# A bias table built in the middle of a down projection, and shorter steps of a layer norm

## The chip, the cores and the metric

The kernel runs on one core of a Trainium2 chip. The metric is the device time of one execution in microseconds (us), as the median of several runs. Engines are named as in the profile: PE (TensorE matmuls; PEld is its weight load), DVE (VectorE), ACT (ScalarE), POOL (GpSimd) and SP (SyncE, which issues most DMAs; a q behind an engine's name means its queue of DMA issues).

## The reference

One inference step of a two-layer encoder over 1056 tokens (1024 of a prompt, 32 of a stream) of width 1024. Layer 0 mixes with an mLSTM, layer 1 with attention over chunks of 64 tokens and the 8 chunks before each; both end in a squared-ReLU MLP of width 4096. Each half layer is

```
x <- LayerNorm(ALPHA * x + gate * sublayer(x * (1 + scale) + shift))
```

with scale, shift and gate from a product of a conditioning vector with w_ada (adaLN). The attention of layer 1 adds a relative-position bias, read for each of 16 heads out of a table of 257 values:

```
rel = q_off + jnp.arange(tq)[:, None] - jnp.arange(tk)[None, :]
idx = jnp.clip(rel, -MAX_REL, MAX_REL) + MAX_REL
return table[:, idx].astype(jnp.float32)
```

## The kernel before, in words

**Matmuls.** Weights are split into a high and a low part, and each product is three matmuls (L118, L119, L120; L120 takes the weight's low part). Raw weights come by SP into a ring of three raw buffers (`raw_tile`, L84), ACT casts the high part (L89), DVE subtracts to get the low part (L90).

**Blocks.** Tokens are worked in three blocks, ti = 0, 1, 2, of 384, 384 and 288 tokens.

**The first down** is layer 0's second MLP product, at about 860 to 1232 us of the span. It runs over groups g = 0 to 7 of the hidden width; w_dn_g_f is a weight quarter of a group, and dn_g_fc_t0 is the result for one of 8 column blocks and one token block. One quarter serves two column blocks, 72 matmuls. DVE adds each result to the residual ACX (L1051).

**Beside it** runs `ada_rest` (L1582), which forms layer 1's adaLN vectors on DVE: `ada_wide` loads 1 MB tiles radw by SP and multiplies them into aw (L279 for the first, L277 for the others), transposes (L286) and reduces (L288). At its very end it calls `bias_table` (L346): load the table (tab), reverse and scale it into rev on ACT and DVE, store rev into the DRAM buffer e_d, and store from there a (16, 64, 576) array of shifted rows into the DRAM buffer bias_d, which the attention reads. tab and rev are raw buffers.

**Order.** Such side tasks are Python generators; each yields the microseconds that should go by until its next step, and `Flow` lets them go on as the main stage emits its matmuls. A scheduler then sets the order on each engine. An engine works its list in order, and so does SP with its DMA issues.

**Layer 1's first norm** (`norm`, L907) follows the attention's output projection op_b, which takes the blocks in the order 2, 1, 0. For each block, sums (s_n, sr_n) go through a matmul with ones (mean_n, L929), the mean is subtracted (L942), squares are summed (q_n, qr_n) and go through a second such matmul (var_n, L929), and from it comes the scale w_n (L954 to L959), with which the block is scaled (L961) and modulated (L904 to L909). `norm` yields w[0] before the mean and w[1] before the variance. For layer 1's first norm w is taken from W10 (L884) by `end_out1` (L1983). The weights of layer 1's up projection (w_up) are split beside it.

Of the kernel before, what the change touches and what calls it, by code (L numbers as in the profile page):

```python
# [16 lines left out]
D = 1024  # L17
# [58 lines left out]
def trunk_kernel(ctx: ExitStack, tc: tile.TileContext, a, o):  # L76
    nc = tc.nc
    flow = Flow()
# [5 lines left out]
    def raw_tile(shape, name):  # L84
        return ring.tile(shape, F32, tag="raw", name=name, bufs=3)
# [55 lines left out]
    e_d = dr.tile([16, 640], F32, name="e_d")  # L141
    bias_d = dr.tile([16, 64, 576], F32, name="bias_d")
# [14 lines left out]
    def lng(i):  # L157
        return pt1[:, i * KC:(i + 1) * KC]

    def lnb(i):  # L160
        return pt1[:, 32 + i * KC:32 + (i + 1) * KC]
# [3 lines left out]
    def ada_part(l, i):  # L165
        return ada[:, l * 48 + i * KC:l * 48 + (i + 1) * KC, :]
# [141 lines left out]
    def ada_fix(base, parts):  # L308

        for i, kind in parts:  # L310
            ap = ada[:, base + i * KC:base + (i + 1) * KC, :]
            if kind == "sc":
                nc.vector.tensor_scalar_add(ap, ap, 1.0)
            else:
                nc.vector.tensor_scalar(ap, ap, 1.0, 1.0 / ALPHA, op0=ALU.add, op1=ALU.mult)

    def combine(ni, g, b, sc, sh):

        for cnd in range(2):
            nc.vector.tensor_mul(comb[:, ni, :, 0, cnd], g, sc[:, :, cnd])  # L320
            nc.vector.tensor_mul(comb[:, ni, :, 1, cnd], b, sc[:, :, cnd])
            nc.vector.tensor_add(comb[:, ni, :, 1, cnd], comb[:, ni, :, 1, cnd], sh[:, :, cnd])
# [20 lines left out]
        nc.vector.tensor_copy(hist, tp[:, :24].rearrange("p (j k) -> p k j", j=3))  # L343
        nc.vector.tensor_copy(n0c, tp[:, 24:28])

    def bias_table():  # L346

        tab = raw_tile([16, 257], "tab")
        nc.sync.dma_start(tab, a["rel_bias_b"][0])
        rev = raw_tile([16, 640], "rev")  # L350
        nc.vector.memset(rev[:, 639:640], 0.0)
        nc.scalar.activation(rev[:, 0:447], tab[:, 256:257].broadcast_to([16, 447]), AF.Copy, scale=8.0)
        fwd = tab[:, 65:257]
        nc.vector.tensor_scalar(rev[:, 447:639], bass.AP(fwd.tensor, fwd.offset + 191, [fwd.ap[0], [-1, 192]]),
                                8.0, None, op0=ALU.mult)
        nc.sync.dma_start(e_d, rev)

        nc.sync.dma_start(bias_d, bass.AP(e_d.tensor, e_d.offset + 63, [[640, 16], [-1, 64], [1, 576]]))


    up_cm = tc.tile_pool(name="upool", bufs=1, side="right", reuse_waits="tile")
# [506 lines left out]
    def acc_dma(d, x, out=False):  # L868
        for i in range(0, KC, 4):
            p = [d[:, i:i + 4], x[:, i:i + 4]]  # L870
            nc.sync.dma_start(*(p if out else reversed(p)))
# [7 lines left out]
    ADA_W = (4.5, 4.5, 2.0)  # L879
# [1 line left out]
    TAIL = (1.0, 1.5)  # L881
    W00 = (6.0, 12.0, 0.0, 0.0, 0.0, 3.0)
    W01 = ((4.0, 6.0, 1.0, 1.0, 1.0), (6.0, 8.0, 2.0, 2.0, 2.0), (3.0, 6.0, 0.0, 0.0, 0.0))
    W10 = ((10.0, 12.0, 0.0, 0.0, 0.0, 3.0), (16.0, 14.0, 0.0, 0.0, 0.0, 3.0))  # L884

    def make_layer(acc, pp, uo, cut=None):

# [654 lines left out]
    fwd, rev = (0, 1, 2), (2, 1, 0)  # L1542
# [10 lines left out]
    mm, norm, _, out_proj, _, add_gated_at = make_layer(acc, bank, uap)  # L1553
    combine(0, lng(0), lnb(0), ada_part(0, 4), ada_part(0, 3))
    norms = {}
# [24 lines left out]
        yield from ada_cols(a["w_ada_kv"], 0, 96, 8, mm, tmp_t, ADA_B)  # L1580

    def ada_rest():  # L1582
        yield from ada_wide(a["w_ada"][1], 0, 48, 48, mm, tmp_t, wc_tile, ADA_W)
        yield from ada_wide(a["w_ada_kv"], D, 104, 8, mm, tmp_t, wc_tile, ADA_W)
        ada_fix(48, [(1, "sc"), (2, "g"), (4, "sc"), (5, "g")])
        ada_fix(96, [(1, "sc")])
        combine(1, lng(1), lnb(1), ada_part(1, 1), ada_part(1, 0))
        combine(2, lng(2), lnb(2), ada_part(1, 4), ada_part(1, 3))
        yield
        bias_table()  # L1590

    class L0:
        wups = wup0
# [41 lines left out]
        def down():  # L1635
            flow.finish(norms["ada"])
            norms["ada"] = flow.add(ada_rest(), carry=True)
# [141 lines left out]
    for i, (nb, ns) in enumerate(((3, 0), (3, 0), (2, 1), (0, 3))):  # L1779
        bt = ring.tile([P, 2112], F32, tag="wc", name=f"bias{i}", bufs=6)  # L1780
        b3 = bt[:, :nb * 576].rearrange("p (b j) -> p b j", j=576) if nb else None
        for hd in range(2 if nb else 0):
            h0 = 2 * len(bias) + hd
            nc.sync.dma_start(b3[64 * hd:64 * hd + 64], bias_d[h0:h0 + 2 * nb - 1:2].rearrange("h i j -> i h j"))
        s3 = bt[:, nb * 576:nb * 576 + ns * 544].rearrange("p (b j) -> p b j", j=544) if ns else None
        for r in range(4 if ns else 0):
            h0 = 4 * len(sbias) + r
# [173 lines left out]
    def open_u2(pr):  # L1961
        u2_cm.append(tc.tile_pool(name=f"u2p{pr}", bufs=1, side="right", reuse_waits="tile"))
        u2p[pr] = u2_cm[-1].__enter__()
        u2[pr] = u2p[pr].tile([P, 2, KC, 2 * QN], F32R, tag="u2", name=f"u2_{pr}")

    def u2ap(hl, k, t0, n):
# [5 lines left out]
    mm, norm, norm_out, out_proj, gain_shift, add_gated_at = make_layer(  # L1972
        acc, lambda name: psD.tile([P, 512], F32, tag="mm", name=name, bufs=8), u2ap, 2 * QN)
# [6 lines left out]

    def end_out1(ti):
        t0, n = TBS[ti]
        norms[ti] = flow.add(norm(ti, 2, f"n10_{ti}", W10[ti == rev[-1]], True, lambda ti: acc_dma(  # L1983
            xsp[2][:, :, t0:t0 + n], acc[ti], True)), now=NOW)
        qo_cm[ti].__exit__(None, None, None)
        if ti == 1:
            open_u2(0)
# [6 lines left out]
    def early_up(ti, pr):  # L1994

        if ti == rev[-1] and pr:
            wup1[FIRST[pr - 1]] = up_weights(1, FIRST[pr - 1])
    out_proj([(0,), (1, 2, 3)], rev, wo_get, o_mov, ada_part(1, 2), end_out1, "b", width=[384, 384, 320],
             after_pr=early_up)

# [96 lines left out]
```

## Time and profile before

| | |
|---|---|
| median of 3 runs | 2435.93 us (2434.0 to 2439.79) |
| profiled execution, own time | 2433.89 us |
| its span | 2432.1 us |
| mean granted TensorE clock | 0.993 |
| busy PE, DVE, ACT, POOL | 97%, 81%, 48%, 7% of the span |
| first down's last groups | PE idle 2.03 us in 1180 to 1232 us |
| layer 1's first norm | PE idle 4.20 us in 1690 to 1730 us |

A row of the timeline has the start in us, the duration in us, the engine, the line, the operation, what it writes and reads with the shapes, and how many such are merged; in brackets stands the idle time before it and what ended it. A row of the waits has who waited for whom, the total in us, how often, and the longest. In the view of DMAs, "under 512 B" and so on count packets by size, and q1 is SP's ring.

### The profile page before, as it was taken

Reading aid. Unit: us, or ns where it says so; the run is one execution under the profiler, and the core shown is the slowest. Engines: PE = TensorE matmul, PEld = TensorE weight load, DVE = VectorE, ACT = ScalarE, POOL = GpSimd, SP = SyncE. Lnnn points to the kernel's source line nnn. Section 1 sums busy time; section 2 is a strip of 40 time slices with the busy share of each in tenths; the row PEclk is TensorE's granted clock in tenths of the full one; section 3 lists DMA queues with packets and bytes.
Section 4 is the critical chain, followed back from the end, with each engine's and each line's share of the span. In section 5 each row is a group of like instructions: output and inputs, shape, how many; then the busy total and the mean of one; then the engine's idle time right before and its main releaser. Section 6 shows DMA issues by size and latency. Waiting matters only on the chain.

```text
span 2432.1 us, 44293 instructions
## 1 busy us (share of the span) xinstructions
PE 2361.3 (97%) x17180; PEld 2265.0 (93%) x17180; DVE 1973.5 (81%) x4094; ACT 1179.6 (48%) x2394; POOL 166.8 (7%) x315
## 2 busy tenths in 40 slices
PE   7999999999999999999999989999999999899997
PEld 4999999999999999999989977889999999899997
DVE  4898997778788789999697666755998888887778
ACT  4654456377666620010157566763776777222212
POOL 0211100000000000000001134420000000000003
PEclk9999999999999999999999999999999999999999
DMA  8433323436556897656423220051486779966642
GB/s 296 122 112 96 101 88 99 143 114 219 179 188 192 294 346 265 234 203 231 145 67 95 74 64 1 15 135 32 163 282 229 256 259 339 364 243 232 227 151 72
DMA packets 283702, 423.60 MB, mean 174 GB/s; under 512 B 15320, under 2 KB 205164, under 8 KB 278372
## 3 DMA queue, kind: packets, MB, share of 16 engines
q1 hardware_dynamic: 279460, 390.50, 48.1%
q10 hardware_dynamic: 4032, 30.28, 3.1%
q8 instruction: 135, 2.21, 0.4%
q14 instruction: 75, 0.61, 0.1%
HBM read 304.91 MB, written 118.17 MB: 174 GB/s over the span
## 4 chain that ended last, share of the span: by engine, by line
PE 48%; DVE 12%; ACT 4%; DMA 3%; issue 2%; POOL 0%; SPq 0%; DVEq 0%; ACTq 0%; POOLq 0%
PE dn L1421 11%; PE up L1286 8%; PE dn L120 5%; PE dn L119 5%; PE dn L118 5%; PE pv L1859 3%; PE s L1802 2%; PE pt L1837 2%; DVE wf_u L90 1%; DVE HL L90 1%; DMA rdn_u<-in_w_up_dram 1%; PE op_b L118 1%; PE op_b L119 1%; PE op_b L120 1%; PE q L119 1%
## 5 line engine op out<-in xcount | busy, mean ns | idle before, releaser
L1051 DVE SCALAR_TENSOR_TENSOR ACX<-dn,ada,ACX 128x264 f32<-128x264 f32 (+6 forms) x664 | 281.8, 447 | 87.9 <-PE dn L1421 42.5
L1421 PE MATMUL dn<-fx,wf_d 128*128 128x264 f32 x2016 | 255.3, 286 | 6.0 <-DVE ACX L1051 3.7
L1421 PEld LDWEIGHTS dn<-fx,wf_d 128*128 128x128 f32 x2016 | 250.2, 189 | 8.1 <-DVE ACX L1051 2.3
L89 ACT CAST w_dn<-raw_dn 128x1024 fp32r<-128x1024 f32 x36 | 37.7, 1051 | 282.8 <-DVE aw L277 159.5
L118 PE MATMUL dn<-hs,w_dn 128*128 128x384 f32 (+2 forms) x512 | 161.3, 315 | 0.8 <-DVE ACX L1051 0.7
L119 PE MATMUL dn<-hs,w_dn 128*128 128x384 f32 (+2 forms) x512 | 160.9, 315 | 0.0
L120 PE MATMUL dn<-hs,w_dn 128*128 128x384 f32 (+2 forms) x512 | 155.9, 314 | 1.8 <-DVE w_dn L90 1.8
L1286 PE MATMUL up<-TF,wf_u 128*128 128x264 f32 x1056 | 143.4, 285 | 3.0 <-ACT H L1289 3.0
L1286 PE MATMUL up<-U,wf_u 128*128 128x264 f32 x1056 | 139.6, 285 | 1.5 <-DVE H L1292 1.1
L1286 PE MATMUL up<-u,wf_u 128*128 128x264 f32 x1056 | 139.7, 285 | 1.2 <-ACT wf_u L89 0.6
L277 DVE SCALAR_TENSOR_TENSOR aw<-radw,cs,aw 128x512 f32<-128x512 f32 x196 | 139.5, 744 | 0.0
L1286 PEld LDWEIGHTS up<-TF,wf_u 128*128 128x128 f32 x1056 | 134.3, 188 | 4.1 <-ACT H L1289 4.0
L1286 PEld LDWEIGHTS up<-U,wf_u 128*128 128x128 f32 x1056 | 133.0, 188 | 2.6 <-DVE H L1292 1.9
L1286 PEld LDWEIGHTS up<-u,wf_u 128*128 128x128 f32 x1056 | 132.6, 188 | 2.2 <-ACT wf_u L89 0.8
L119 PE MATMUL dn<-U,w_dn 128*128 128x384 f32 (+2 forms) x416 | 129.8, 313 | 0.0
L118 PE MATMUL dn<-U,w_dn 128*128 128x384 f32 (+2 forms) x416 | 129.3, 311 | 0.0
L120 PE MATMUL dn<-U,w_dn 128*128 128x384 f32 (+2 forms) x416 | 125.5, 312 | 0.6 <-DVE w_dn L90 0.6
L120 PEld LDWEIGHTS dn<-hs,w_dn 128*128 128x128 f32 x512 | 95.8, 188 | 2.9 <-DVE w_dn L90 2.6
L118 PEld LDWEIGHTS dn<-hs,w_dn 128*128 128x128 f32 x512 | 96.4, 188 | 1.4 <-DVE ACX L1051 1.0
L119 PEld LDWEIGHTS dn<-hs,w_dn 128*128 128x128 f32 x512 | 96.4, 188 | 0.0
L1812 DVE CUSTOM_DVE_ANT_0 p<-s,bias 128x576 f32<-128x576 f32 (+9 forms) x132 | 79.0, 606 | 19.6 <-PE s L1802 12.8
L90 DVE TENSOR_TENSOR HL<-H,HL 128x1056 fp32r<-128x1056 f32 x64 | 80.2, 1254 | 17.5 <-ACT HL L89 17.4
(394 smaller groups left out, 7163.4 us busy)
## 6 DMA issues: line engine op xcount, KB each, us to landing
hpl<-HL SPq DMA_DIRECT2D x144, 264.0 KB
rdn_u<-in_w_up_dram SPq DMA_DIRECT2D x64, 512.0 KB
hd<-HL SPq DMA_DIRECT2D x28, 1056.0 KB
fx<-hd SPq DMA_DIRECT2D x50, 528.0 KB
radw<-in_w_ada_dram SPq DMA_DIRECT2D x24, 1024.0 KB
hd<-HM SPq DMA_DIRECT2D x28, 792.0 KB
raw_up<-in_w_up_dram SPq DMA_DIRECT2D x40, 512.0 KB
raw_dn<-in_w_down_dram SPq DMA_DIRECT2D x36, 512.0 KB
```

The lines of the kernel that those rows point to most:

```text
L90: (eng or nc.vector).tensor_sub(dst_l, src, dst_h.bitcast(F32))
L118: nc.tensor.matmul(ps, wh, mov(0, k), start=(k == 0), stop=False)
L119: nc.tensor.matmul(ps, wh, mov(1, k), start=False, stop=False)
L120: nc.tensor.matmul(ps, wl, mov(0, k), start=False, stop=(k == nk - 1))
L277: nc.vector.scalar_tensor_tensor(acc[cnd], raw[:, k], sc, acc[cnd], op0=ALU.mult, op1=ALU.add)
L1051: nc.vector.scalar_tensor_tensor(xs, ps[:, off + o:off + o + mm_], gate[:, fc, cnd:cnd + 1], xs, op0=ALU.mult, op1=ALU.add)
L1286: nc.tensor.matmul(p, self.ws[w][:, wl, k], moving(f, tp, xl, k), start=first and k + n_ == 0, stop=k == 3 and n_ == 2, skip_group_check=n ...
L1421: nc.tensor.matmul(p, ws[w][:, wl, k], t[:, s0, xl], start=first and k + n_ == 0, stop=k == kg - 1 and n_ == 2, skip_group_check=not first)
L1802: nc.tensor.matmul(s[:, b, :w], qst, kk[i][:, g, k0 + j0:k0 + j0 + w], start=(i == 0), stop=(i == 1))
L1812: nc.vector.tensor_tensor_reduce(out=z.rearrange("p (b w) -> p b w", b=np_), in0=s[:, :np_, :w], in1=bt.rearrange("p (b w) -> p b w", b=np ...
L1837: nc.tensor.transpose(pt[:kp, j - j0, pr * P:(pr + 1) * P], ps_[pr][:, j * P:j * P + kp], ident)
L1859: nc.tensor.matmul(pv[64 * e:64 * e + 64, :nq], V[:kp, vt0 + j, g * 64:(g + 1) * 64], pts[e][:kp, j, :nq], start=(j == 0), stop=(j == nt - 1))
```

## The change

`ada_rest` now forms layer 1's 48 adaLN columns in two calls of `ada_wide` with `bias_table` between them, which puts the table into the middle of the first down. `bias_table` is a generator with yields, takes tab and rev from the pool of temporary tiles instead of the raw ring, and stores bias_d in four DMAs of four heads. W10 has an entry for each block: block 0 keeps its steps, block 1 goes from (10, 12) to (9, 10), and block 2 from (10, 12) to (6, 8). Lines behind L358 move by two or three.

```diff
-    def bias_table():
+    def bias_table(tmp_f):
 
-        tab = raw_tile([16, 257], "tab")
+        tab = tmp_f([16, 257], "tab")
         nc.sync.dma_start(tab, a["rel_bias_b"][0])
-        rev = raw_tile([16, 640], "rev")
+        yield 2.0
+        rev = tmp_f([16, 640], "rev")
...
         nc.sync.dma_start(e_d, rev)
-
-        nc.sync.dma_start(bias_d, bass.AP(e_d.tensor, e_d.offset + 63, [[640, 16], [-1, 64], [1, 576]]))
+        for h0 in range(0, 16, 4):
+            yield 1.0
+            nc.sync.dma_start(bias_d[h0:h0 + 4], bass.AP(e_d.tensor, e_d.offset + 640 * h0 + 63,
+                                                         [[640, 4], [-1, 64], [1, 576]]))
...
-    W10 = ((10.0, 12.0, 0.0, 0.0, 0.0, 3.0), (16.0, 14.0, 0.0, 0.0, 0.0, 3.0))
+    W10 = ((16.0, 14.0, 0.0, 0.0, 0.0, 3.0), (9.0, 10.0, 0.0, 0.0, 0.0, 3.0), (6.0, 8.0, 0.0, 0.0, 0.0, 3.0))
...
     def ada_rest():
-        yield from ada_wide(a["w_ada"][1], 0, 48, 48, mm, tmp_t, wc_tile, ADA_W)
+        yield from ada_wide(a["w_ada"][1], 0, 48, 24, mm, tmp_t, wc_tile, ADA_W)
+        yield from bias_table(tmp_t)
+        yield from ada_wide(a["w_ada"][1], 3 * D, 72, 24, mm, tmp_t, wc_tile, ADA_W)
         yield from ada_wide(a["w_ada_kv"], D, 104, 8, mm, tmp_t, wc_tile, ADA_W)
...
-        yield
-        bias_table()
...
-        norms[ti] = flow.add(norm(ti, 2, f"n10_{ti}", W10[ti == rev[-1]], True, lambda ti: acc_dma(
+        norms[ti] = flow.add(norm(ti, 2, f"n10_{ti}", W10[ti], True, lambda ti: acc_dma(
```

What the change does to the order is shown at three places. The first is SP's list around groups 3 and 4 of the first down. A row has the line, the operation, what is written and read (a tile's name ends in a number of the program), and the shape. Before:

```order
L96 DMA raw_dn_3_2_11898<-in_w_down_dram 128x4x256
L261 DMA radw_28_1_11808<-in_w_ada_dram 128x4x512
L261 DMA radw_32_0_11892<-in_w_ada_dram 128x4x512
L96 DMA raw_dn_3_3_12013<-in_w_down_dram 128x4x256
L261 DMA radw_32_1_12005<-in_w_ada_dram 128x4x512
L96 DMA raw_dn_4_0_12114<-in_w_down_dram 128x4x256
L261 DMA radw_36_0_12093<-in_w_ada_dram 128x4x512
L96 DMA raw_dn_4_1_12231<-in_w_down_dram 128x4x256
```

The same stretch now, in which the second `ada_wide` counts its tiles from 0 again:

```order
L96 DMA raw_dn_3_2_11891<-in_w_down_dram 128x4x256
L261 DMA radw_4_0_11803<-in_w_ada_dram 128x4x512
L349 DMA tab<-in_rel_bias_b_dram 16x257
L96 DMA raw_dn_3_3_12000<-in_w_down_dram 128x4x256
L357 DMA e_d<-rev 16x640
L360 DMA bias_d<-e_d 256x1x576 x4
L261 DMA radw_4_1_11910<-in_w_ada_dram 128x4x512
L261 DMA radw_8_0_11994<-in_w_ada_dram 128x4x512
L261 DMA radw_8_1_12107<-in_w_ada_dram 128x4x512
L96 DMA raw_dn_4_0_12115<-in_w_down_dram 128x4x256
L96 DMA raw_dn_4_1_12224<-in_w_down_dram 128x4x256
```

The table's load and stores stand ahead of three adaLN tiles and of group 4's weights, and raw_dn_4_0 has moved behind three adaLN tiles instead of one. At the end of the first down the rows tab, e_d and bias_d, which stood among raw_dn_6_3 to raw_dn_7_1, are gone.

The second place is DVE's list ahead of the split of w_dn_4_0, where dn_3_7 is the last column block of group 3. Before:

```order
L277 SCALAR_TENSOR_TENSOR aw_32_1_12008<-radw_32_1_12005,cs,aw_32_1_12008 128x512
L1051 SCALAR_TENSOR_TENSOR ACX_1_10263<-dn_3_7_0_12065,ada,ACX_1_10263 128x384
L90 TENSOR_TENSOR w_dn_4_0_12116<-raw_dn_4_0_12114,w_dn_4_0_12116 128x1024
L1051 SCALAR_TENSOR_TENSOR ACX_1_10263<-dn_3_7_384_12079,ada,ACX_1_10263 128x384
L277 SCALAR_TENSOR_TENSOR aw_32_0_12007<-radw_32_1_12005,cs,aw_32_0_12007 128x512
```

And now, with the products of radw_8_0 ahead of the split:

```order
L1054 SCALAR_TENSOR_TENSOR ACX_1_10263<-dn_3_7_384_12066,ada,ACX_1_10263 128x384
L277 SCALAR_TENSOR_TENSOR aw_8_0_12109<-radw_8_0_11994,cs,aw_8_0_12109 128x512
L277 SCALAR_TENSOR_TENSOR aw_8_1_12110<-radw_8_0_11994,cs,aw_8_1_12110 128x512
L1054 SCALAR_TENSOR_TENSOR ACX_1_10263<-dn_3_7_768_12086,ada,ACX_1_10263 128x256
L1054 SCALAR_TENSOR_TENSOR ACX_1_10263<-dn_3_7_768_12086,ada,ACX_1_10263 128x32
L302 TENSOR_TENSOR ada<-adas_6_12101,pt_86 128x16
L90 TENSOR_TENSOR w_dn_4_0_12117<-raw_dn_4_0_12115,w_dn_4_0_12117 128x1024
```

The split has moved from behind the first add of dn_3_7 to behind the last one. On PE the first matmul with the low part of w_dn_3_3 now stands three matmuls behind the end of dn_3_5, and the first with the low part of w_dn_4_0 sixteen behind the end of dn_3_7; in the order of before, matmuls of neighbouring quarters were interleaved more deeply there.

The third place is PE's list in layer 1's output projection, around block 2's variance; op_b_1 is a result of block 1, op_b_0 one of block 0. Before:

```order
L120 MATMUL op_b_1_18724<-QO_14264,w_ob_1_18398 128x384
L929 MATMUL var_n_2_18750<-qr_n_2_18669,ones_d 128x288 x2
L118 MATMUL op_b_0_18787<-QO_13933,w_ob_0_18175 128x384
L119 MATMUL op_b_0_18787<-QO_13933,w_ob_0_18175 128x384
L120 MATMUL op_b_0_18787<-QO_13933,w_ob_0_18175 128x384
```

And now:

```order
L120 MATMUL op_b_1_18675<-QO_14267,w_ob_1_18198 128x384
L932 MATMUL var_n_2_18701<-qr_n_2_18646,ones_d 128x288 x2
L118 MATMUL op_b_1_18725<-QO_14267,w_ob_0_18395 128x384
L119 MATMUL op_b_1_18725<-QO_14267,w_ob_0_18395 128x384
L120 MATMUL op_b_1_18725<-QO_14267,w_ob_0_18395 128x384
```

Block 2's variance has moved from behind block 1's last product into the middle of block 1's, 48 matmuls further forward, and its mean 24; block 1's mean and variance stand at the same counts as before.

## The prediction

> **What bounds the kernel now.** I read the page's busy table first, then the busy time of the engines by stretches, then the waits of the two stretches that the change touches, and last the timelines of VectorE (DVE) and of the queue that issues DMAs (SP).
>
> ```profile
> PE 2361.3 (97%) x17180; PEld 2265.0 (93%) x17180; DVE 1973.5 (81%) x4094; ACT 1179.6 (48%) x2394; POOL 166.8 (7%) x315
> ```
> ```profile
> 1010.00:1060.00 50.00, 49.45 (x309) 48.57 (x309) 48.29 (x87) 5.26 (x5) 0.00 (x0) 1.00 0.67 243
> 1060.00:1110.00 50.00, 49.41 (x310) 48.67 (x309) 48.24 (x86) 4.20 (x4) 0.00 (x0) 1.00 0.64 233
> ...
> 1180.00:1200.00 20.00, 19.29 (x119) 18.97 (x118) 6.87 (x14) 3.15 (x3) 0.00 (x0) 1.00 0.46 132
> 1200.00:1232.00 32.00, 30.68 (x176) 30.07 (x175) 24.63 (x34) 8.15 (x11) 0.00 (x0) 1.00 0.27 82
> ...
> 1690.00:1730.00 40.00, 35.80 (x232) 35.46 (x231) 38.87 (x68) 29.40 (x57) 0.00 (x0) 0.96 0.36 109
> ...
> 1760.00:1790.00 30.00, 30.00 (x246) 29.82 (x245) 29.97 (x42) 24.31 (x38) 0.00 (x0) 1.00 0.78 264
> ```
>
> In the second fence the columns are the stretch, its length, then busy time and count of PE, PEld, DVE, ACT and POOL, and last the granted clock, the DMA share and GB/s. PE is busy for 2361.3 of 2432.1 us, so some 71 us of idle time in all can be won, and anything that makes PE wait costs its full length. The change touches three places. In the middle of the first down (1010 to 1110) PE idles only 0.55 + 0.59 us, but DVE is at 97%: what DVE does there is already tight, and 0.16 us (49.45 / 309) is the time of a matmul. At the first down's end (1180 to 1232) PE idles 0.71 + 1.32 us and DVE is two thirds idle in the first part. At layer 1's first norm (1690 to 1730) PE idles 4.20 us.
>
> **End of the first down: the table goes away.** The two waits there, and what SP and DVE do before them:
>
> ```profile
> PE dn L120 <- DVE w_dn L90: 1.3, 1, 1.3
> PE dn L118 <- DVE ACX L1051: 0.7, 1, 0.7
> ```
> ```profile
> 1144.27 0.34 SPq L349 DMA_DIRECT2D tab<-in_rel_bias_b_dram  x1
> 1166.55 0.38 SPq L96 DMA_DIRECT2D raw_dn<-in_w_down_dram  x1
> 1172.47 0.33 SPq L356 DMA_DIRECT2D e_d<-rev  x1
> ...
> 1174.20 0.60 SPq L358 DMA_DIRECT2D bias_d<-e_d  x1
> 1174.85 6.89 SPq L96 DMA_DIRECT2D raw_dn<-in_w_down_dram  x3
> 1203.24 8.67 SPq L96 DMA_DIRECT2D raw_q<-in_w_q_b_dram  x5
> ```
> ```profile
> 1201.46 0.62 DVE L1051 SCALAR_TENSOR_TENSOR ACX<-dn,ada,ACX 128x384 f32<-128x384 f32 x1 [2.47 <-PE dn L120]
> 1201.99 3.49 DVE L90 TENSOR_TENSOR w_dn<-raw_dn,w_dn 128x1024 fp32r<-128x1024 f32 x3
> ```
>
> The last three down weights are split on DVE only at 1201.99, behind an add that waits for PE, and PE waits for the first of them. With the table gone, raw_dn_6_3 no longer waits for one of the three raw buffers, of which tab and rev held two, no store stands between the last raw loads, and in the new order all four splits of the last group stand ahead of the adds of dn_6_7. So both waits fall: -2.0 us (from -2.0 to 0, if DVE's delayed adaLN products fill the gap). What is late next is nothing that the rows show before the norm of layer 0, whose own waits I leave as they are.
>
> **Middle of the first down: what comes in.** The table's four steps stand on SP behind radw_4_0, and on DVE the table's one product stands behind the adds of dn_2_6:
>
> ```profile
> 991.89 0.37 SPq L96 DMA_DIRECT2D raw_dn<-in_w_down_dram  x1
> ```
> ```profile
> 998.93 0.64 DVE L1051 SCALAR_TENSOR_TENSOR ACX<-dn,ada,ACX 128x256 f32<-128x256 f32 x2
> ...
> 1040.92 0.64 DVE L1051 SCALAR_TENSOR_TENSOR ACX<-dn,ada,ACX 128x256 f32<-128x256 f32 x2
> ...
> 1041.55 1.22 DVE L90 TENSOR_TENSOR w_dn<-raw_dn,w_dn 128x1024 fp32r<-128x1024 f32 x1
> 1042.68 2.07 DVE L277 SCALAR_TENSOR_TENSOR aw<-radw,cs,aw 128x512 f32<-128x512 f32 x3
> ...
> 1051.92 0.61 DVE L1051 SCALAR_TENSOR_TENSOR ACX<-dn,ada,ACX 128x384 f32<-128x384 f32 x1
> ...
> 1057.27 1.29 DVE L286 STREAM_TRANSPOSE awt<-aw 128x512 f32<-128x512 f32 x2
> ...
> 1059.01 1.26 DVE L288 TENSOR_REDUCE cx<-awt 128x16 f32<-128x512 f32 x2
> ...
> 1060.96 0.88 DVE L279 TENSOR_SCALAR aw<-radw,cs 128x512 f32<-128x512 f32 x2
> ```
>
> After raw_dn_3_2 (991.9) and radw_4_0 the tab load goes out at about 993; DVE comes to rev at about 999.5 (998.93 + 0.64), so its wait for tab is 0 to 1 us and is covered, since the next w_dn split that PE needs is ten microseconds ahead. From e_d's store to the bias store took 1.7 us (1172.47 to 1174.20), so the first of the four goes out at about 1002.5. While SP waits for e_d, radw_4_1, radw_8_0, radw_8_1 and raw_dn_4_0 stand behind it.
>
> Three costs follow. First, w_dn_3_3: PE has three matmuls in hand there (0.5 us), and its split stands right behind the last adds of dn_3_5. These adds and the split take 0.6 + 1.2 us, so PE waits 1.3 us. The order of before had dozens of other matmuls in hand.
>
> Second, w_dn_4_0. From that split on DVE has 8 aw products (5.5 us at 2.07 for three), six add groups (3.2), transposes 1.25, reduces 1.2, 0.85 for L279, two more products 1.4, 0.1 for L302 and the split 1.2: 14.7 us. PE has 72 matmuls of w_dn_3_3 and sixteen that need only w_dn_4_0's first half, less one: 87 x 0.16 = 13.9 us. That is a wait of 0.8 us. The two waits of 1.1 us that stood in 1010 to 1110 belong to an order that is gone; others like them may come, so I credit half, -0.5.
>
> Third, radw_4_1, which DVE wants at about 1042 (behind the split at 1041.55). Every microsecond by which it lands later is one more for w_dn_4_0 and so for PE, since DVE works in order.
>
> ```profile
> DMA packets 16, 0.00 MB, mean 21 GB/s; under 512 B 8, under 2 KB 16, under 8 KB 16
> ```
> ```profile
> DMA packets 1138, 5.45 MB, mean 389 GB/s; under 512 B 79, under 2 KB 79, under 8 KB 626
> ...
> U<-hpl ACTq DMA_DIRECT2D x3, 1056.0 KB
> radw<-in_w_ada_dram SPq DMA_DIRECT2D x3, 1024.0 KB
> ```
> ```profile
> DMA packets 1669, 3.00 MB, mean 300 GB/s; under 512 B 29, under 2 KB 651, under 8 KB 1668
> ...
> q1 hardware_dynamic: 1668, 2.98, 99.1%
> ```
>
> The first of these is the stretch 1.6 to 1.8, in which the c_rows load of 8 rows of 512 bytes arrived: 8 data packets and 8 small ones that close it. The second is 1004 to 1018, with U's loads (four in all), the third 1176 to 1186, half of it the bias store of before, whose source has 16 outer steps and which kept the queue's 16 engines 99.1% busy. If the engines of a transfer follow its outer count, as 8 closing packets for 8 rows suggest, each of the new stores, with 4 outer steps, runs on 4 engines, all on the same. [...]
>
> On such an engine stand, from 1002.5 on: a quarter of 1024 x 2304 bytes (590 KB), a sixteenth of the four U loads (270 KB) and of radw_4_1 (66 KB), 926 KB. At the rate of the second stretch, 389 / 16 = 24.3 KB a us, that takes 38 us and radw_4_1 lands at 1040.6: no cost. At the third's, 300 / 16 = 18.8, it takes 49.2 us, lands at 1051.7 and costs 9.7. I take 1.5 us, near the faster end, because the same U loads make up that stretch and only four engines write. The middle costs 1.3 + 0.8 - 0.5 + 1.5 = 3.1 us (from 0 to 11.3).
>
> **The norm's shorter steps.**
>
> ```profile
> PE var_n L929 <- ACT qr_n L89: 4.2, 1, 4.2
> ```
> ```profile
> 1672.09 2.74 DVE L942 TENSOR_TENSOR ACC<-ACC,mean_n 128x576 f32<-128x576 f32 x4
> ...
> 1678.60 0.46 DVE L90 TENSOR_TENSOR qr_n<-q_n,qr_n 128x288 fp32r<-128x288 f32 x1 [0.56 <-ACT qr_n L89]
> 1680.14 0.62 DVE L1043 SCALAR_TENSOR_TENSOR ACC<-op_b,ada,ACC 128x384 f32<-128x384 f32 x1 [1.08 <-PE op_b L120]
> 1684.30 0.62 DVE L1043 SCALAR_TENSOR_TENSOR ACC<-op_b,ada,ACC 128x384 f32<-128x384 f32 x1 [3.55 <-PE op_b L120]
> 1686.20 0.46 DVE L957 SCALAR_TENSOR_TENSOR w_n<-var_n,w_n 128x288 f32<-128x288 f32 x1 [1.28 <-ACT w_n L956]
> ...
> 1703.07 0.95 DVE L942 TENSOR_TENSOR ACC<-ACC,mean_n 128x768 f32<-128x768 f32 x1
> ...
> 1714.52 0.55 DVE L90 TENSOR_TENSOR qr_n<-q_n,qr_n 128x384 fp32r<-128x384 f32 x1
> ```
>
> PE's 4.2 us are one wait, for the squares of block 1, ready at about 1714. DVE had idled 1.08 + 3.55 + 1.28 = 5.9 us before 1686.2, because block 2's var matmul came late, and then did block 2's scaling just when block 1's squares were due: the subtraction of block 1's mean begins only at 1703.07. In the new order block 2's mean stands 24 matmuls further forward and its var 48: its w_n comes about 8 us earlier, its scaling fills those 5.9 us, and block 1's chain, at the same matmuls as before, moves forward by about as much. Its squares are then ready at about 1714.5 - 5.9 = 1708.6, and PE, which comes to them 4.2 us before 1714, at about 1709.8, does not wait. Block 2's own var stands some 50 matmuls behind its mean now, 8 us at 0.16, and the chain between them took 7 (1672.09 to 1678.60 + 0.46), so it has its squares in time. That is -4.2 us (from -4.2 to 0). What is late next is DVE itself, with 29.97 of 30 us from 1760 on; it comes there some 5 us earlier too, so I count no return.
>
> **The sum.** -2.0 + 3.1 - 4.2 = -3.1 us. The profiled execution of before took 2433.9 us (span 2432.1 and 1.8 around it), which gives 2430.8; the median of the runs shown is 2435.9, 2.0 above the profiled one, so I forecast 2432.8 as a median.
>
> **The rivals.** About 0.2%, 4.9 us, is what a measurement of this kernel can tell from no change.
>
> *The stores are hidden.* They run on 16 engines, or on 4 at 24.3 KB a us, radw_4_1 is in time, and w_dn_4_0 is too, since DVE has gaps earlier in that group. Then the middle costs 0.5 us: -5.7, or 2430.2. For it: DMA share is only 0.67 in 1010 to 1060. Against it: the wait for w_dn_3_3 stands in the order itself.
>
> *The stores hold the next weights: slower.* Four engines move the stores at 18.8 KB a us or less, radw_4_1 lands at 1051.7 or later and DVE, with the adds of dn_3_6 behind that product, stops for 9.7 us: the middle costs 11.3, the sum is +5.1 and the time 2441.0, up to 2446 at 17 KB a us. It decides once radw_4_1 lands after about 1051.5. For it: the third stretch is the only one with such a store. Against it: that one shares its engines with three weight loads.
>
> *The norm's wait comes back.* Block 1's squares stay behind the splits of w_up on DVE, or PE's 4.2 us are lost again where DVE is full (1760 to 1790). Then -2.0 + 3.1 = +1.1, or 2437.0. For it: DVE at 38.87 of 40 us. Against it: the 5.9 us of holes.
>
> **How the numbers follow.** Forecast 0.36, hidden 0.26, slower 0.20, norm back 0.18. The hidden case and 0.10 of the forecast's, at its lower end, lie over 4.9 us below 2435.9: faster 0.36. Slower is that rival, 0.20, the rest 0.44 is the same. The range goes from 2427, the hidden case with no cost at all in the middle and some 2 to 3 us more from the norm waits behind the first down, to 2441, and leaves out most of the slower rival.
>
> **What would show it.** Right: no wait of PE for qr_n in 1690 to 1760, no wait on w_dn at about 1200, one of 1 to 3 us for w_dn_3_3 and w_dn_4_0 between 1038 and 1058, and radw_4_1 landing within 2 us of 1042. Wrong: over 5 us of PE idle in 1010 to 1110 (the late load), or PE idle of 3 us and more in 1690 to 1830 (the norm).

## The result and the profile after

| | before | after |
|---|---|---|
| median | 2435.89 us (2432.43 to 2441.47, 16 runs) | 2429.07 us (2424.62 to 2434.35, 16 runs) |
| profiled execution, own time | 2433.89 us | 2430.01 us |
| its span | 2432.1 us | 2427.9 us |
| mean granted clock | 0.993 | 0.993 |

The ratio after to before is 0.9968, with a 95% interval of 0.996 to 0.9977: 5.6 to 9.7 us less, more than what a measurement of this kernel can tell from no change. The forecast was 2432.8 us in a range of 2427 to 2441.

First the busy time by the stretches shown in the prediction, now of the changed kernel. The columns are the same: stretch, length, busy time and count of PE, PEld, DVE, ACT and POOL, granted clock, DMA share, GB/s.

```profile
1010.00:1060.00 50.00, 48.31 (x304) 47.45 (x302) 41.85 (x84) 4.05 (x4) 0.00 (x0) 1.00 0.73 267
1060.00:1110.00 50.00, 49.58 (x310) 48.74 (x309) 48.49 (x86) 5.26 (x5) 0.00 (x0) 1.00 0.61 219
1180.00:1200.00 20.00, 20.00 (x133) 19.72 (x132) 17.62 (x43) 3.81 (x4) 0.00 (x0) 1.00 0.50 157
1200.00:1232.00 32.00, 32.00 (x185) 32.00 (x184) 20.82 (x30) 5.42 (x9) 0.00 (x0) 1.00 0.06 18
1690.00:1730.00 40.00, 40.00 (x275) 40.00 (x274) 38.45 (x67) 27.66 (x51) 0.00 (x0) 1.00 0.33 102
```

PE has no idle time left at the first down's end (before 0.71 + 1.32) nor at layer 1's norm (before 4.20), and it has 1.69 us of it in 1010 to 1060 (before 0.55). At the norm the count tells more than the idle time: 275 matmuls where 232 stood.

The profiled spans differ by 4.2 us only, because the profiled execution of after started slower: its first 5800 matmuls, which the change does not touch, took 4 us more. PE has the same 17180 matmuls in every kernel here, and in the same order but for a few short runs of them, none of which lies at a bound used here. So a stretch between two matmuls by count can be compared between kernels free of that. Such stretches carry most of what follows (us, worked out from the starts of PE's instructions in each trace):

| stretch, by count of matmuls | what lies there | before | after | difference |
|---|---|---|---|---|
| 1 to 5800 | nothing changed | 830.7 | 834.8 | +4.0 |
| 5800 to 6600 | first down, ahead of the table's first step in after | 105.95 | 105.86 | -0.1 |
| 6600 to 8200 | middle of the first down, with the table in after | 255.35 | 256.34 | +1.0 |
| 8200 to 8250 | end of the first down | 11.35 | 8.78 | -2.6 |
| 8250 to 11500 | up to the norm of layer 1 | 493.6 | 493.6 | 0.0 |
| 11500 to 11600 | norm of layer 1, block 1 | 21.3 | 15.3 | -6.0 |
| 11600 to the end | | 699.7 | 698.8 | -0.9 |
| 5800 to the end | | 1587.3 | 1578.7 | -8.6 |

The first row is scatter: in the other twelve kernels of this study it lies between 829.2 and 835.4. So is the last but one, which lies between 698.6 and 700.4. The middle and the end are sharp: 255.35 to 255.38 us in the seven kernels that have the table later, and 8.78 in all nine that have no wait in the end's stretch.

**The middle.** SP's part of the timeline of after, and then DVE's (start, duration, engine, line, operation, count, idle time before and what ended it):

```profile
1005.28 0.33 SPq L357 DMA_DIRECT2D e_d<-rev  x1
1006.95 19.05 SPq L360 DMA_DIRECT2D bias_d<-e_d  x4
1026.10 13.96 SPq L261 DMA_DIRECT2D radw<-in_w_ada_dram  x3
1040.11 5.05 SPq L96 DMA_DIRECT2D raw_dn<-in_w_down_dram  x2
```
```profile
1004.62 0.25 DVE L355 TENSOR_SCALAR rev<-tab 16x192 f32<-16x192 f32 x1 [0.77 <-DMA tab<-in_rel_bias_b_dram]
...
1036.01 0.62 DVE L1054 SCALAR_TENSOR_TENSOR ACX<-dn,ada,ACX 128x384 f32<-128x384 f32 x1 [1.49 <-PE dn L120]
...
1043.96 1.22 DVE L90 TENSOR_TENSOR w_dn<-raw_dn,w_dn 128x1024 fp32r<-128x1024 f32 x1
1046.02 3.40 DVE L277 SCALAR_TENSOR_TENSOR aw<-radw,cs,aw 128x512 f32<-128x512 f32 x5 [0.84 <-DMA radw<-in_w_ada_dram]
...
1059.10 1.21 DVE L90 TENSOR_TENSOR w_dn<-raw_dn,w_dn 128x1024 fp32r<-128x1024 f32 x1
```

SP issues the four stores at 1006.95, and three adaLN tiles stand behind them until 1026.10. SP itself is held there: in the trace the third store's issue takes 14.1 us, and the issue of radw_4_1 behind them 8.3, until 1034.4. From 1033 on DVE has only adds that wait for PE: it has run out of adaLN tiles. radw_4_1 comes at about 1046, and DVE waits for it for 0.84 us. And this is how the DMA engines spent 1006 to 1034 (the first two lines are 40 slices of 0.7 us: mean busy share in tenths of the 16 engines, and GB/s):

```profile
DMA  2006599999999999999722222222222222222222
GB/s 59 0 0 82 168 392 337 379 382 437 419 418 418 421 445 428 413 391 442 273 114 95 108 111 95 101 99 102 105 102 105 99 105 102 105 102 102 102 102 105
...
q10 hardware_dynamic: 576, 4.33, 39.3%
q1 hardware_dynamic: 680, 1.51, 14.2%
```

While U's loads run (ring q10) all 16 engines are busy. Then, for 14 us, only the bias stores are left, and the engines stand at "2" with 102 GB/s: a quarter of the 16 engines works (a share of 0.26, 103 GB/s, in 1021 to 1034). So a store with 4 outer steps did run on 4 engines here; the same bytes with 16 outer steps filled all 16 (e3 below). The waits of PE in 1000 to 1110:

```profile
PE dn L120 <- DVE w_dn L90: 1.8, 3, 1.3
PE dn L118 <- DVE ada L302: 0.3, 1, 0.3
```

The three for w_dn are 1.34 us for w_dn_3_3 at 1045.23, 0.18 for w_dn_4_0 at 1060.36, and 0.24 at 1095.46. The 0.35 stands at 1059.24: a matmul waits for the row of DVE (L302, done at 1059.18) that stands right ahead of w_dn_4_0's split, so it belongs to the same lateness of DVE, 0.53 us in all.

### The profile page after: what moved, and what is told of

The parts are those of the page before. It is cut to its first block, busy times and chain, and to the rows that moved or that the text cites. A ratio compares the mean times of both kernels' runs of the same rounds, so it can differ in the third digit from the quotient of the medians.

```text
span 2427.9 us, 44306 instructions
## 1 busy us (share of the span) xinstructions
PE 2361.4 (97%) x17180; PEld 2265.5 (93%) x17180; DVE 1973.8 (81%) x4094; ACT 1180.5 (49%) x2394; POOL 166.5 (7%) x315
## 4 chain that ended last, share of the span: by engine, by line
PE 50%; DVE 10%; DMA 4%; ACT 4%; issue 2%; POOL 1%; SPq 0%; ACTq 0%; DVEq 0%; POOLq 0%
PE dn L1424 11%; PE up L1289 8%; PE dn L120 4%; PE dn L119 4%; PE dn L118 4%; PE pv L1862 3%; PE s L1805 2%; PE pt L1840 2%; DMA radw<-in_w_ada_dram 2%; PE op_b L118 1%; PE op_b L119 1%; DVE wf_u L90 1%; PE op_b L120 1%; DMA rdn_u<-in_w_up_dram 1%; PE up L120 1%
```

## The experiments

Each diff is against the changed kernel; an edit that an earlier experiment has shown is named in words. Ratios are against the kernel before, in runs on the same chip.

### The three parts apart

**e1: the norm's steps alone.** The table is back at the end, in the raw ring and one store.

```diff
-        yield from ada_wide(a["w_ada"][1], 0, 48, 24, mm, tmp_t, wc_tile, ADA_W)
-        yield from bias_table(tmp_t)
-        yield from ada_wide(a["w_ada"][1], 3 * D, 72, 24, mm, tmp_t, wc_tile, ADA_W)
+        yield from ada_wide(a["w_ada"][1], 0, 48, 48, mm, tmp_t, wc_tile, ADA_W)
...
+        yield
+        bias_table()
```

> Only W10 is changed; the bias table stays at the first down's end. Theory (three separate terms): PE's 4.2 us wait for qr_n in 1690 to 1760 is gone, the two waits at about 1200 (2.0 us) stay, the middle of the first down stays at 1.1 us idle: 4.2 us below the kernel before, some 2431.7 as a median. Rival (the norm's gain comes only with the shift that the table's move brings, or is given back where DVE is full): idle of 3 us or more in 1690 to 1850, and the time within 1 us of before.

Measured: 0.9972 (0.9962 to 0.9983), median 2431.72. The norm's stretch takes 15.3 us, the end 11.34, as before.

**e2: the table alone.** W10 as before.

```diff
-    W10 = ((16.0, 14.0, 0.0, 0.0, 0.0, 3.0), (9.0, 10.0, 0.0, 0.0, 0.0, 3.0), (6.0, 8.0, 0.0, 0.0, 0.0, 3.0))
+    W10 = ((10.0, 12.0, 0.0, 0.0, 0.0, 3.0), (16.0, 14.0, 0.0, 0.0, 0.0, 3.0))
```

> Only the table is moved (middle of the first down, temporary tiles, four stores); W10 is that of before. Theory: the waits at about 1200 are gone (-2.0), the middle costs about 1 us more than before, the norm's wait of 4.2 us stays: 1.0 us below before, not to be told from it. Rival (the table's move brings most of the gain): 4 us or more below before.

Measured: 0.9988 (0.9978 to 0.9998), median 2433.42. The middle takes 255.99 us, the end 8.78, the norm 21.1 with its wait of 4.1 us. The two parts, -0.28% and -0.12%, make up the whole (-0.32%) within their intervals: they don't touch each other.

**e3: the stores on 16 engines.** Each of the four stores takes 16 of the 64 shifts for all 16 heads, so that it has 16 outer steps.

```diff
-        for h0 in range(0, 16, 4):
+        for r0 in range(0, 64, 16):
             yield 1.0
-            nc.sync.dma_start(bias_d[h0:h0 + 4], bass.AP(e_d.tensor, e_d.offset + 640 * h0 + 63,
-                                                         [[640, 4], [-1, 64], [1, 576]]))
+            nc.sync.dma_start(bias_d[:, r0:r0 + 16], bass.AP(e_d.tensor, e_d.offset + 63 - r0,
+                                                             [[640, 16], [-1, 16], [1, 576]]))
```

> The changed kernel, with the four stores of the bias table cut along the 64 rows (16 heads x 16 rows each) instead of along the heads: the same bytes, but 16 outer steps on both sides. Theory (a transfer's engines follow its outer count): the stores run on all 16 engines and end some 20 us earlier, DVE does not wait for radw_4_1, and PE's wait for w_dn_4_0 (0.35 us) goes, while the 1.3 us for w_dn_3_3 stay, since they stand in the order: 0.3 to 0.6 us below the changed kernel. Rival (the stores are slow because they go from DRAM to DRAM in strided rows): about 100 GB/s for 20 us as with four engines, and no difference.

Measured: 0.9963 (0.9951 to 0.9976), median 2427.74. SP's rows, and the slices of 1000 to 1036 (0.9 us each):

```profile
1002.14 2.65 SPq L360 DMA_DIRECT2D bias_d<-e_d  x4
1006.25 21.89 SPq L261 DMA_DIRECT2D radw<-in_w_ada_dram  x3
```
```profile
DMA  4201899999999999999999999999721079999991
GB/s 140 57 0 15 302 361 290 262 304 364 410 434 430 421 414 434 414 429 424 430 413 393 391 411 405 405 405 405 282 89 39 0 100 330 412 396 379 352 339 41
```

The four issues take 2.65 us instead of 19.05, and the engines are full until the stores and U's loads are done at about 1026. PE's waits at w_dn_4_0 (0.35 and 0.18) and DVE's for radw_4_1 (0.84) are gone; the 1.34 for w_dn_3_3 stands, at 1041.21. The middle takes 255.42 us, 0.4 to 1.0 less than in the four kernels with stores on 4 engines (255.84 to 256.46), and 0.1 more than before. In the time of the whole kernel the gain is within the interval of after's own ratio, so by that this version can't be called faster than the changed kernel.

### The norm: which step, and how much slack

**e5 and e6: block 2's steps alone, block 1's alone.** The table stands as in e1.

```diff
+    W10 = ((16.0, 14.0, 0.0, 0.0, 0.0, 3.0), (10.0, 12.0, 0.0, 0.0, 0.0, 3.0), (6.0, 8.0, 0.0, 0.0, 0.0, 3.0))   # e5
+    W10 = ((16.0, 14.0, 0.0, 0.0, 0.0, 3.0), (9.0, 10.0, 0.0, 0.0, 0.0, 3.0), (10.0, 12.0, 0.0, 0.0, 0.0, 3.0))   # e6
```

> The kernel before with W10 shortened for block 2 alone, to (6, 8); block 1 keeps (10, 12), the table stays at the end. Theory (block 1's squares were late because block 2's scaling fell on DVE at that time): the 4.2 us wait is gone, and with it the stretch from PE's 11,500th to its 11,600th matmul falls from 21.3 to 15.3 us: about 6 us below before, as with all of W10. Rival (block 1's own shorter steps bring it): the wait of 4.2 us stays and the time is that of before.

> The kernel before with W10 shortened for block 1 alone, to (9, 10); block 2 keeps (10, 12). Theory: PE's order around block 2 is that of before, so the wait for block 1's squares stays at 4 us, and the time is that of before. Rival (block 1's own steps bring it): about 6 us below before.

Measured: e5 0.997 (0.9958 to 0.9982), the norm's stretch 15.3 us; e6 0.9998 (0.999 to 1.0007), the stretch 21.0. The waits of PE in 1690 to 1765, of e6 (e5 has none):

```profile
PE var_n L929 <- ACT qr_n L89: 4.1, 1, 4.1
```

Block 2's steps bring all of it, though the wait that goes is block 1's: DVE does block 2's scaling earlier and is free for block 1's squares.

**e7 and e8: block 1's squares made later,** by one and by three additions on DVE whose result nothing uses.

```diff
+            if nm == "n10_1":
+                pad = t2("pad")
+                for _ in range(3):      # e7: range(1)
+                    nc.vector.tensor_add(pad, q0, q0)
```

> The changed kernel with one more DVE addition of 128 x 768 (into a tile that nothing reads) ahead of block 1's squares in layer 1's first norm; the order puts one w_up split there too, so PE should wait 1 to 2 us for qr_n again. Theory (a short wait costs its length, a long one lowers the granted clock to 0.5 for about 3 us behind it as well, as after the 4.2 us wait of before): granted clock 1.00 in the 3 us behind the wait, and PE's 11,500th to 11,600th matmul in 15.3 us and the wait. Rival (the clock falls behind each wait): 0.5 for 3 us, and 1.8 us more than the wait.

> As the kernel with one addition, but with three; the order puts two splits there, so PE should wait 4 to 6 us. Theory: the granted clock falls to about 0.5 for some 3 us behind the wait, and PE's 11,500th to 11,600th matmul take 15.3 us, the wait and 1.5 to 2 us more. Rival (the lost time behind the 4.2 us wait of before had another cause, such as DVE's order there): no more than the wait.

Measured: e7 (one run) shows no wait and a stretch of 15.55 us: the squares had that much slack, more than the theory gave them. e8 (one run) has the wait back. Its waits and its busy time by 3 us stretches, and then the same stretches behind the wait in the kernel before:

```profile
PE var_n L932 <- ACT qr_n L89: 2.9, 1, 2.9
```
```profile
1709.00:1712.00 3.00, 3.00 (x16) 3.00 (x17) 0.94 (x2) 0.81 (x2) 0.00 (x0) 0.64 0.55 172
1712.00:1715.00 3.00, 3.00 (x22) 3.00 (x22) 2.01 (x4) 1.21 (x3) 0.00 (x0) 0.79 0.14 50
1715.00:1718.00 3.00, 3.00 (x27) 3.00 (x26) 3.00 (x8) 2.54 (x6) 0.00 (x0) 1.00 0.00 0
```
```profile
1714.00:1717.00 3.00, 2.94 (x12) 2.92 (x13) 3.00 (x5) 1.07 (x4) 0.00 (x0) 0.51 0.81 214
1717.00:1720.00 3.00, 3.00 (x25) 3.00 (x25) 2.20 (x4) 1.80 (x4) 0.00 (x0) 0.93 0.76 234
```

PE is busy in all of them, and yet it does 16 or 12 matmuls in 3 us where 27 go at a clock of 1.00. e8's stretch took 19.96 us: 15.28, the wait of 2.86, and 1.82 more. Before's 21.30 is 15.28, the wait of 4.20, and again 1.82 more. So a wait here costs its length and 1.8 us of lower clock behind it. In the four other kernels with this wait (4.1 us in e2, e4, e6 and e9) it is 1.7 to 2.2 us.

### The end: buffers, stores or order

**e4: the table stays at the end, in one store, but in pool tiles** instead of the raw ring; W10 as in e2.

```diff
         yield from ada_wide(a["w_ada_kv"], D, 104, 8, mm, tmp_t, wc_tile, ADA_W)
+        yield
+        bias_table(tmp_t)
```

> The kernel before, with tab and rev taken from the temporary tiles instead of the raw ring; the table stays at the first down's end, with its one store, and W10 is that of before. Theory (the late weights of the last group come from the raw buffers that tab and rev hold): raw_dn_6_3 goes out some 15 to 20 us earlier, the last splits come before 1195 and both waits at about 1200 go: 2.0 us below before. Rival (the store of 2.3 MB ahead of the last weights, or SP's wait for e_d, is what makes them late): the waits stay, 1.3 to 2 us, and the time is that of before.

Measured: 1.0014 (1.0005 to 1.0023), median 2440.95: this theory failed. The first of the two waits (0.71) is gone, the second comes one weight quarter (72 matmuls) later, and a larger one has come with layer 0's norm. SP's row of the table, PE's longest waits in 1180 to 1290 and the clock behind the new one:

```profile
1168.73 0.49 SPq L349 DMA_DIRECT2D tab<-in_rel_bias_b_dram  x1
```
```profile
PE var_n L929 <- ACT qr_n L89: 6.6, 1, 6.6
PE dn L120 <- DVE w_dn L90: 1.3, 1, 1.3
```
```profile
1266.00:1272.00 6.00, 4.39 (x12) 3.62 (x12) 5.75 (x11) 2.39 (x6) 0.00 (x0) 0.50 0.26 87
```

So taking the table out of the raw ring brought no more than the 0.71 there. That the squares came 6.57 us late goes with splits of w_q that now stand ahead of them on DVE; this was read from the order, and not tried by itself.

**e9: the table at its old place, the old ring, but stored in four** by heads, as the change has it; W10 as in e2.

```diff
-        nc.sync.dma_start(bias_d, bass.AP(e_d.tensor, e_d.offset + 63, [[640, 16], [-1, 64], [1, 576]]))
+        for h0 in range(0, 16, 4):
+            nc.sync.dma_start(bias_d[h0:h0 + 4], bass.AP(e_d.tensor, e_d.offset + 640 * h0 + 63,
+                                                         [[640, 4], [-1, 64], [1, 576]]))
```

(This diff is against the kernel before.)

> The kernel before with nothing changed but its one store of the bias table, which is cut into four of four heads at its old place at the first down's end, ahead of raw_dn_7_1. Theory (four outer steps, four engines, 103 GB/s): the stores take about 23 us from 1175 on, the shares of raw_dn_7_1 to raw_dn_7_3 on those engines land only behind them, at 1200 to 1206, and PE's waits at about 1200 grow from 2.0 to 5 to 9 us: 4 to 9 us above before. Rival (the stores cost nothing where they stand, as the split order holds the weights anyway): the time of before.

Measured: 1.0013 (1.0004 to 1.0023), median 2439.68, so 1 to 6 us above before, less than was expected. The slices of 1178 to 1206 (0.7 us each), the waits of PE in 1180 to 1240 and the clock behind:

```profile
DMA  3222222222222222222224989659839982222100
GB/s 119 102 102 105 95 89 66 92 104 95 99 99 105 105 105 105 95 102 105 105 105 112 173 319 332 161 168 356 313 121 238 336 300 97 97 95 94 50 19 0
```
```profile
PE dn L118 <- ACT w_dn L89: 2.4, 1, 2.4
PE dn L118 <- DVE ACX L1053: 0.7, 1, 0.7
```
```profile
1206.00:1210.00 4.00, 4.00 (x15) 4.00 (x14) 2.57 (x4) 1.91 (x2) 0.00 (x0) 0.50 0.73 226
```

The same four engines at 102 GB/s hold the last weights until the matmuls need them: the end's stretch takes 15.4 us, 6.6 more than with no table there. The store on 4 engines, which cost the middle little, costs the end 4.1 us more than the store on 16.

### Other places for the table

All three take e3's stores and the new W10.

**e10: during the query projection of layer 1,** started as a task of its own when the second group of it begins.

```diff
+            if gi == 1 and ti == 0:
+                flow.add(bias_table(tmp_t))
```

> The changed kernel with the bias table built later instead: adaLN in one call as before, the table as a task of its own from the last part of the q projection on (at about 1290 us; the attention reads it at 1402), stores cut along the rows with 16 outer steps, W10 as changed. Theory: the first down's middle is that of before (no 1.3 us for w_dn_3_3, -1 us), the end's and the norm's gains stay (3.0 and 6.0 us): 1 us below the changed kernel, 8 to 10 below before. Rival (the q projection or the key stage has no room for the table's steps): idle there above before's 5.3 and 8.8 us, and no gain over the changed kernel.

**e11: at the start of the first down,** ahead of all of layer 1's adaLN columns.

```diff
+        yield from bias_table(tmp_t)
+        yield from ada_wide(a["w_ada"][1], 0, 48, 48, mm, tmp_t, wc_tile, ADA_W)
```

> The table is built ahead of all of layer 1's adaLN columns, at the very start of the first down, its stores cut along the 64 shifts (16 outer steps each), and the shorter norm steps stay. Theory (the table costs only where its steps change the order of a tight stretch, and its removal from the end is worth 3.0 us wherever it goes ahead of the end): PE from matmul 7400 to 8250 in 135.7 us against 138.6 of before, 11500 to 11600 in 15.3 against 21.3, and the middle (5800 to 7400) within 0.5 us of before's 234.0: together 8.5 to 9 us below before, 2427.0, ratio 0.9965. Rival (the start of the first down is as full as the middle, or the stores push the first down weights back): PE waits of 2 us and more for w_dn of group 0 or 1 (850 to 900 us), and 2429 to 2433.

**e12: in layer 0's up stage,** behind the first eight adaLN columns of w_ada_kv, which belong to layer 1's attention (the text below calls them layer 0's).

```diff
     def ada_some():
         yield from ada_cols(a["w_ada_kv"], 0, 96, 8, mm, tmp_t, ADA_B)
+        yield from bias_table(tmp_t)
```

> The table is built still earlier, in layer 0's up stage between two parts of layer 0's adaLN columns, its stores cut along the 64 shifts, and the shorter norm steps stay; ada_rest runs in one piece of 48 columns again. Theory (as for the table first): the first down has no step of the table left, its middle costs nothing more than before (5800 to 7400 in 234.0 us), its end 135.7 and the norm 15.3, so 9 us below before, 2426.8, ratio 0.9963. Rival (every place has its price, since SP works in order and the table's steps hold what stands behind them): a new PE wait of 1 to 5 us in the up stage, 700 to 860 us, for a weight split or an adaLN column, and 2428 to 2432.

Measured: e10 0.9986 (0.9977 to 0.9994), e11 1.0042 (1.0028 to 1.0056), e12 1.0032 (1.0021 to 1.0044). The theory failed in all three. What it said of the old places held: the end took 8.78 us in all three, the norm 15.3. But each new place has its own wait, and those of e11 and e12 are far larger than their rivals said. The longest waits of PE in e10, e11 and e12, each from its own trace:

```profile
PE kv L1755 <- DVE x L1734: 5.0, 1, 5.0
```
```profile
PE dn L120 <- DVE w_dn L90: 18.0, 2, 17.2
```
```profile
PE dn L118 <- ACT w_dn L89: 12.6, 1, 12.6
```

In e10 the lists of SP and DVE show why. The loads of x stand behind the table's stores, so POOL, which takes x first, begins at 1333.39 (before 1325.72) and is done with it by 1337.2. But DVE makes its product of x only at 1348.68: it stands in order behind products of q (L1686) that wait for PE, and DVE idles up to 2.56 us before each. In before it was made from 1328.74 on.

```profile
1319.44 2.91 SPq L360 DMA_DIRECT2D bias_d<-e_d  x4
1322.45 3.58 SPq L1728 DMA_DIRECT2D x<-xsp  x2
```
```profile
1333.39 3.77 POOL L1733 TENSOR_TENSOR x<-x,kvss 128x1024 f32<-128x1024 f32 x2 [965.14 <-DMA x<-xsp]
```
```profile
1340.23 0.55 DVE L1686 TENSOR_TENSOR QO<-q,QO 64x384 fp32r<-64x384 f32 x1 [2.56 <-ACT QO L1685]
...
1348.68 2.36 DVE L1734 TENSOR_TENSOR x<-x,kvss 128x1024 f32<-128x1024 f32 x2
```

For e11 the first row below is the stretch 870 to 910 of the kernel before, in which the DMA share is 0.97; then e11's rows of SP, and of DVE in front of the late split:

```profile
870.00:910.00 40.00, 40.00 (x334) 39.53 (x332) 40.00 (x77) 5.18 (x5) 0.00 (x0) 1.00 0.97 357
```
```profile
877.07 6.97 SPq L360 DMA_DIRECT2D bias_d<-e_d  x3
884.28 1.87 SPq L261 DMA_DIRECT2D radw<-in_w_ada_dram  x2
```
```profile
899.61 0.88 DVE L279 TENSOR_SCALAR aw<-radw,cs 128x512 f32<-128x512 f32 x2 [9.28 <-DMA radw<-in_w_ada_dram]
900.41 6.71 DVE L277 SCALAR_TENSOR_TENSOR aw<-radw,cs,aw 128x512 f32<-128x512 f32 x10
907.03 1.22 DVE L90 TENSOR_TENSOR w_dn<-raw_dn,w_dn 128x1024 fp32r<-128x1024 f32 x1
```

DMA had nothing to spare there. The adaLN tiles go out behind the stores and arrive at 899.6, DVE stands still for 9.28 us, and the split that PE needs, whose weight ACT had cast by 890.8, stands behind ten products of those tiles. In e12 it is the weight itself that comes late. How much of either is the full engines and how much SP's order was not taken apart.

What the table costs PE by its place (the stretch in which it stands, against the kernels that have no table there):

| place | stores | longest new wait | cost, us |
|---|---|---|---|
| end of the first down (before) | one, 16 engines | 1.3 | 2.6 |
| end of the first down (e9) | four, 4 engines | 2.4 | 6.6 |
| middle of the first down (after) | four, 4 engines | 1.3 | 1.0 |
| middle of the first down (e3) | four, 16 engines | 1.3 | 0.1 |
| layer 1's kv projection (e10) | four, 16 engines | 5.0 | 6.7 |
| start of the first down (e11) | four, 16 engines | 17.2 | about 19 |
| layer 0's up stage (e12) | four, 16 engines | 12.6 | about 17 |

The middle's cost is that of matmuls 6600 to 8200: 256.34 us in after, and 255.99, 256.46 and 255.84 in e2, e7 and e8, whose stores are the same. It is a net: new waits come there, and two old ones (0.55 and 0.59) go. The cost of e10 is that of 9050 to 9120, 16.1 us against 9.3 in all other kernels. For e11 and e12 it is that of 5800 to 8200, 380.4 and 378.4 us against 360.7 to 362.3 in the seven kernels that have the table later; part of e12's table stands ahead of matmul 5800.

## Why the prediction came out as it did

**The norm, -6.0 for -4.2: right in mechanism, and too small.** The wait is gone, and e5 shows that block 2's steps do it, as the prediction argued from DVE's 5.9 us of holes. The changed kernel's rows: block 1's mean is subtracted from 1700.21 (before 1703.07), and its squares are done at 1711.0 (1710.48 + 0.56; before 1715.1).

```profile
1700.21 3.53 DVE L945 TENSOR_TENSOR ACC<-ACC,mean_n 128x768 f32<-128x768 f32 x4
...
1710.48 0.56 DVE L90 TENSOR_TENSOR qr_n<-q_n,qr_n 128x384 fp32r<-128x384 f32 x1
```

That is 4.0 us earlier by the two traces, and 6.6 against PE's count, since matmul 11500 starts at 1702.3 in after and at 1699.6 in before; 5.9 had been forecast. The 1.8 us on top are the clock: the prediction priced a wait of PE at "its full length", and its own row of 1690 to 1730 stood at a granted clock of 0.96 without being read.

**The end, -2.6 for -2.0: right, and a little too small.** Both waits are gone wherever the table leaves the end (e2, e3, e10, e11, e12). Three reasons were given: the raw buffers, the store ahead of the last weights, and the order of DVE's splits. The rows of before speak for the third: the weights were not late there, ACT had cast all of the last three by 1193.1,

```profile
1192.06 1.05 ACT L89 CAST w_dn<-raw_dn 128x1024 fp32r<-128x1024 f32 x1 [0.39 <-DMA raw_dn<-in_w_down_dram]
```

and DVE, idle up to 1.5 us between its adds, split them only at 1201.99, behind an add that waits for PE. In e4 three of the last four splits come by 1181.2; the fourth, whose weight was cast by 1191.3, stands at 1215.42, behind such an add again, and PE waits for it. In after all four splits of the last group are done by 1194.0, the last of them starting at

```profile
1192.74 1.23 DVE L90 TENSOR_TENSOR w_dn<-raw_dn,w_dn 128x1024 fp32r<-128x1024 f32 x1
```

The order alone, with the table left in place, was not tried. The waits were 2.03 us and the clock 1.00; the remaining 0.5 us of the stretch no row explains.

**The middle, +1.0 for +3.1: the steps were right, the terms for w_dn_4_0 and the credit were mis-sized.** The wait for w_dn_3_3 was to be 1.3 and is 1.34. The stores did run on 4 engines, as the prediction took it when no run had shown a transfer of 4 outer steps: the trace of after has a share of 0.26 of the 16 engines while they are alone. That all four stores take the same 4 was the author's estimate; no view names a packet's engine, but a share that stays at 0.26 fits it. In after PE runs 4.2 us later here for reasons that lie ahead of the change (matmul 6800 starts at 974.6 instead of 970.4); taken off, the stores start at 1002.7 (forecast 1002.5) and radw_4_1 comes at about 1041.8 (1040.6 by the faster rate, 1051.7 by the slower one). The rate is 926 KB an engine in 39.1 us, from 1006.95 to 1046.02: 23.7 KB a us, near the upper bound of 24.3. So the tile cost DVE 0.84 us and not 1.5. The sum for w_dn_4_0 was 14.7 us of DVE's work and 1.5 of lateness against 13.9 of PE's: 2.3 us. From the end of one split (1045.18) to the end of the next (1060.31) DVE needed 15.1 us with its 0.84 idle, so 14.3 of work, and PE, which went on at 1045.23 and had w_dn_4_0 at 1060.36, was idle 0.53 of these 15.1 and so had 14.6 of work. All three parts were sized a little against the change. The credit of 0.5 was too small: before's 0.55 and 0.59 went, and 0.24 came, 0.9 net. So 1.34 + 0.53 - 0.90 is 0.97 us, and the stretch says 0.99.

**The sum and the chances.** -2.6 + 1.0 - 6.0 is -7.6 us; the stretches from 5800 on give -8.6, the medians -6.8 and the interval -5.6 to -9.7, where the forecast said -3.1. The range held it, in part by luck: its lower end counted on a middle that costs nothing and on 2 to 3 us from the norm waits behind the first down, but 8250 to 11500 took the same 493.6 us, and what came was the clock behind layer 1's norm. The most likely single outcome, a change within 0.2%, did not come: all three terms were off in the same direction. The nearest rival, the hidden stores with 2430.2, came closer to the time and to the way: 4 engines near 24.3 KB a us and a tile almost in time. Its middle at 0.5 us lies between the 0.1 of e3, with 16 engines, and the 1.0 of after; its -2.0 and -4.2 were the same mis-sized terms. The slower rival's condition (landing after 1051.5) was not met in the middle; e11 shows its mechanism at a place where it does decide. The norm's wait did not come back.

## What to carry to other kernels

A side task's price is set by the place that it is put in: read there the DMA share, the queue that it is put into, and what stands behind it on each engine in order, before you compare its own cost at the old and the new place; here one table cost 1 us or 19. A PE wait can cost clock behind it as well, as the 2.43 us of e9 did (0.50 behind them): read that from the granted clock and the count of matmuls in the stretches that follow. And see whether a late step waits for its data or for its place in its engine's list: at the first down's end and in e10 the data had long been there. And a wait is often removed at another block than the one that waits: look for what fills the engine in front of it.

## What the runs showed of the hardware

**The clock fell after short waits already, but not after each.** Granted clock in the stretch behind a wait of PE: 1.00 behind 0.71 and 1.3 us (the ends of before and e4, the middle of after), 0.50 behind 2.43 (e9), 0.50 behind 2.86 (e8, 1709.9 to 1713.3), 0.51 behind 4.20 (before, 1714.0 to 1717.4), 0.50 for 10 us behind 6.57 (e4). At layer 0's norm eight kernels have the same wait of 2.7 to 2.8 us for a split of w_q: behind it the clock was 0.50 for 3.4 us in after, e7, e8, e10 and e11, and stayed at 1.00 in e2, e3 and e12. In before and in e8 the price was 1.8 us each, whatever the length of the wait; 3.4 us at half clock are 1.7 of it.

**The stores of four outer steps moved 102 GB/s.** Alone, the stores by heads ran at about 102 GB/s, in the middle (after) and at the end (e9); cut along 16 steps (e3), stores and U's loads together ran at 391 to 434 (1009 to 1025). Beside U's loads the stores got little: of the 5.86 MB that 1006 to 1034 moved, 4.33 were on U's ring, which was nearly through by 1020; the stores went on by themselves for 14 us more.
